# One step of a delta-rule recurrence: the key norm by one wide matmul, masks in wide operations, two heads in turn

## The chip, the cores and the metric

The kernel runs on one core of a Trainium2 chip. The metric is the device time of one execution, in microseconds (us). The kernel before was run three times: 3231.21, 3232.57 and 3237.78 us, with 3232.57 as the median. One further execution was recorded by the hardware profiler; every row below comes from it.

## The reference

A trunk of two layers over 2048 tokens of width 1024, in float32. Layer A is a time-mixing layer with a state of 64 x 64 for each of 12 heads. Layer B is differential attention with 6 heads. Both have a small cross-attention into 256 memory tokens beside them, a gate, an output projection and norms. The change touches layer A alone. What is computed there for every token, cut to what matters:

```
w = -softplus(-(w0 + tanh(wd) @ w2)) - 0.5;  decay = exp(-exp(w))
a = sigmoid(a0 + ad @ a2)
kk = k * k_k;  kk = kk * rsqrt(max(sum(kk * kk, per head), 1e-12))
k = k * (1 + (a - 1) * k_a)
# for each head, token by token:
sa = state @ (-kk)
state = state * decay + sa (kk * a)^T + v k^T
y = state @ r
```

Each head's key direction `kk` is brought to length one (the key norm), and it enters twice: once as `kk` itself and once as `b = kk * a`.

## The kernel before, in words

Layer A goes through 24 steps: two halves of 1024 tokens, in each six pairs of heads, and for each pair two blocks of 512 tokens. In a step the two heads of the pair lie on partitions 0 to 63 and 64 to 127, and the 512 tokens are cut into 8 chunks of 64. Within a chunk the recurrence is solved in closed form, and the state goes from chunk to chunk. A step is traced in these parts.

- p1 (line 312): projections of key, query and value, each 24 matmuls of 128x512 (`pj`, line 174: eight parts of the width, three products of high and low halves); two low-rank products (`lr`, lines 323 and 324: the high part of the weights on all 128 rows, and the low part on 64 of them); decay and gate by exponentials and logarithms on ScalarE, a scan on VectorE (line 330); the key norm (lines 336 to 348); and the tables AR and BK, which hold r, a and k, b of each chunk.
- p2 (line 371): the products `pg` of BK and AR, 64 rows each, for 8 chunks and 2 heads (line 380). A mask for even or odd chunks and the reciprocal norm are put on them on the way out of PSUM (`Gm`, line 383). Then BK is transposed (`bkp`, line 390) and scaled by the reciprocal norm (`BKT`, line 391), and the bonus `pbn` is computed (line 404).
- p3 (line 409): the inverse of a triangular matrix for each chunk and head. Thirty small operations on VectorE solve blocks of 16; two groups of `inv` matmuls (line 455) and the groups `invz` and `invr` (lines 468, 474) join them to 32 and 64.
- p4 (line 482): the recurrence over 8 chunks, one after the other. In a chunk `xy` (lines 493, 496) goes to ScalarE (`xs`), `us` (line 502) to VectorE (`UV`), then come `sps` (line 507), the state's update on VectorE (line 510) and the output `xy` (line 513).
- p5 (line 516): the output's norm, with the transposes `py` (line 535), and its gate.

The scheduler sets the order on every engine when the program is built. While p4 of one step runs, it fills TensorE with the gate projection of that step and the p1 of the step after next (function `filler`, line 584), so `pj` matmuls stand between the short matmuls of p3 and p4. An engine executes its instructions in the order of its row, and whatever waits holds up all that is behind it. The projections, `lr` and `pbn` share three PSUM buffers (tag `pj`); `pg`, `bkp` and the inverse's groups share two others (tag `gm`). The working tiles of 128x512 in SBUF come from eight buffers (tag `w`).

## Time and profile before

| | |
|---|---|
| median of three runs | 3232.57 us |
| lowest and highest run | 3231.21 and 3237.78 us |
| span of the profiled execution | 3242.7 us |
| TensorE (PE) busy | 3074.5 us, 95% |
| VectorE (DVE) busy | 2008.1 us, 62% |
| ScalarE (ACT) busy | 1421.3 us, 44% |
| GpSimd (POOL) busy | 928.4 us, 29% |

The page gives the profiled execution's time as its span, 10.1 us over the median of the other runs. "Busy" is the time in which an engine had at least one instruction in it. Matmuls overlap, and so a TensorE that is busy all the time is not one at its peak. The recorded time of a matmul holds its way through the array too. What one costs in a row of its like is read from start to start.

### The profile page before, as it was taken

How to read it: one execution, taken by the hardware profiler on the slowest of the kernel's cores; microseconds unless marked ns; L12 is line 12 of the kernel's file. 1: busy time of each engine (PE TensorE's matmuls, PEld its weight loads, DVE VectorE, ACT ScalarE, POOL GpSimd, SP SyncE). 2: the span in 40 equal slices, each digit the busy share in tenths (PEclk: the TensorE clock that was granted, in tenths of full speed). 3: DMA queues.
4: the chain of work that ended last, by engine and by line, in shares of the span. 5: the costliest groups of instructions: out<-in, count | busy, mean ns of one | idle time of the engine just before them, and what ended most of it. 6: DMA issues, size and time to landing. Idle time of an engine off the chain costs nothing.

```text
span 3242.7 us, 53751 instructions
## 1 busy us (share of the span) xinstructions
PE 3074.5 (95%) x20026; PEld 2404.1 (74%) x20026; DVE 2008.1 (62%) x5546; ACT 1421.3 (44%) x3126; POOL 928.4 (29%) x1092
## 2 busy tenths in 40 slices
PE   6899999998899999999899999999999999999999
PEld 4766767676667676767577798898887878877777
DVE  6678777866687878786456411111106888887554
ACT  6524333434443434333345522222315777777443
POOL 3224434443244334433100121312411332222100
PEclk9989999998899999999899999999999999999999
DMA  4201000113210001002554443423436555444453
GB/s 131 75 16 35 27 22 22 34 40 90 57 35 27 23 22 33 29 18 69 136 147 135 134 113 90 117 74 96 117 110 159 118 116 112 102 85 119 118 154 113
DMA packets 266150, 265.21 MB, mean 82 GB/s; under 512 B 16832, under 2 KB 206656, under 8 KB 265760
## 3 DMA queue, kind: packets, MB, share of 16 engines
q1 hardware_dynamic: 237760, 195.31, 20.7%
q0 software_dynamic: 28128, 66.46, 10.1%
q8 instruction: 157, 2.57, 0.3%
q14 instruction: 105, 0.86, 0.1%
HBM read 180.45 MB, written 81.26 MB: 81 GB/s over the span
## 4 chain that ended last, share of the span: by engine, by line
PE 76%; DVE 14%; ACT 4%; issue 3%; DMA 2%; POOL 1%; SPq 0%; DVEq 0%; ACTq 0%; POOLq 0%
PE pj L174 30%; PE po L820 10%; PE o L1135 5%; PE vps L996 4%; PE pg L380 3%; PE s L1094 3%; PE s L1095 2%; PE us L502 2%; PE xy L496 2%; PE tr L1125 2%; PE sps L507 1%; PE xy L493 1%; PE mo L759 1%; PE xy L513 1%; DVE E L1097 1%
## 5 line engine op out<-in xcount | busy, mean ns | idle before, releaser
L174 PE MATMUL pj<-hhi,wh 128*128 128x512 f32 x928 | 395.3, 426 | 2.2 <-DVE hlo L149 1.7
L174 PE MATMUL pj<-hhi,wl 128*128 128x512 f32 x928 | 393.2, 424 | 0.4 <-POOL wl L123 0.4
L174 PE MATMUL pj<-hlo,wh 128*128 128x512 f32 x928 | 385.0, 415 | 0.0
L123 POOL TENSOR_TENSOR wl<-wraw,wh 128x512 fp32r<-128x512 f32 x168 | 221.0, 1327 | 399.8 <-ACT wh L122 372.2
L1097 DVE CUSTOM_DVE_ANT_0 E<-s,dist 128x512 f32<-128x512 f32 (+1 forms) x480 | 276.2, 605 | 35.0 <-PE s L1095 28.9
L174 PE MATMUL pj<-bh,wh 128*128 128x512 f32 x672 | 262.6, 391 | 0.0
L174 PE MATMUL pj<-bl,wh 128*128 128x512 f32 x672 | 262.4, 391 | 0.0
L174 PE MATMUL pj<-bh,wl 128*128 128x512 f32 x672 | 262.3, 390 | 0.0
L1102 ACT ACTIVATE E<-E,nm 128x1920 f32<-128x1920 f32 (+7 forms) x192 | 229.4, 1199 | 59.1 <-DVE nm L1100 58.6
L491 POOL TENSOR_SCALAR SP<-sb,PC 128x128 f32<-128x128 f32 x192 | 119.5, 624 | 469.7 <-DVE sb L510 469.7
L1135 PE MATMUL o<-th,vs 128*128 128x256 f32 (+1 forms) x864 | 211.0, 376 | 2.3 <-ACT th L1128 0.9
L174 PEld LDWEIGHTS pj<-hhi,wh 128*128 128x128 f32 x928 | 178.5, 192 | 45.6 <-ACT hhi L148 3.3
L1094 PE MATMUL s<-ks,qd 128*128 128x512 f32 (+1 forms) x480 | 205.7, 432 | 2.2 <-DVE mx L1097 1.2
L174 PEld LDWEIGHTS pj<-hhi,wl 128*128 128x128 f32 x928 | 177.6, 191 | 38.9 <-POOL wl L123 0.8
L174 PEld LDWEIGHTS pj<-hlo,wh 128*128 128x128 f32 x928 | 178.2, 192 | 33.9 <-issue 0.2
L122 ACT ACTIVATE wh<-wraw 128x512 fp32r<-128x512 f32 x168 | 105.4, 628 | 198.0 <-PE pj L174 138.9
L1135 PEld LDWEIGHTS o<-th,vs 128*128 128x128 f32 x864 | 153.8, 189 | 38.7 <-ACT th L1128 19.4
L514 ACT ACTIVATE ys<-xy 64x128 f32<-64x128 f32 x192 | 52.0, 271 | 297.0 <-PE xy L513 251.5
L1095 PE MATMUL s<-ks,qd 128*128 128x512 f32 (+1 forms) x480 | 176.2, 373 | 0.0
L510 DVE SCALAR_TENSOR_TENSOR sb<-sps,PC,SP 64x64 f32<-64x64 f32 x384 | 108.4, 282 | 64.9 <-PE sps L507 57.0
L174 PEld LDWEIGHTS pj<-bh,wh 128*128 128x128 f32 x672 | 126.6, 188 | 26.4 <-DVE ot L831 0.3
L174 PEld LDWEIGHTS pj<-bl,wh 128*128 128x128 f32 x672 | 126.6, 188 | 26.2
(401 smaller groups left out, 7342.3 us busy)
## 6 DMA issues: line engine op xcount, KB each, us to landing
wraw<-in_a_w SPq DMA_DIRECT2D x126, 256.0 KB, 2.9
qd<-qd_d POOLq DMA_DIRECT2D x48, 512.0 KB, 6.9
mq<-mq POOLq DMA_DIRECT2D x64, 256.0 KB, 4.3
ks<-ks_d POOLq DMA_DIRECT2D x24, 512.0 KB, 6.5
yr<-y_dram SPq DMA_DIRECT2D x31, 384.0 KB, 4.9
xt<-in_x SPq DMA_DIRECT2D x16, 512.0 KB, 5.3
x_dram<-ot SPq DMA_DIRECT2D x16, 512.0 KB, 4.4
wraw<-in_b_w SPq DMA_DIRECT2D x32, 256.0 KB, 3.0
```

Source lines behind the costliest of these rows:

```text
L122: A.activation(hi[:, ks], raw, AF.Copy)
L123: eng.tensor_tensor(out=lo[:, ks], in0=raw, in1=hi[:, ks].bitcast(F32), op=ALU.subtract)
L174: mm(ps, lhsT=w[a_][:, k, wcol], rhs=h[b_][:, k, tsl], start=n == 0, stop=n == 3 * KT - 1)
L491: G_.tensor_scalar(out=SP, in0=SB, scalar1=PC[:, c:c + 1], scalar2=None, op0=ALU.mult)
L510: V.scalar_tensor_tensor(out=SB[hc, hc], in0=sp[hc, :], scalar=PC[hc, c:c + 1], in1=SP[hc, hc], op0=ALU.mult, op1=ALU.add)
L820: mm(po[hf], lhsT=a_[:, k, :], rhs=b_[hf][:, k, :], start=k == i == 0, stop=k == KT - 1 and i == 2)
L996: mm(ps[:, t, :], lhsT=hT[b][a_][:, k, tsl], rhs=w[b_][:, k, :], start=n == 0, stop=n == 3 * KT - 1)
L1094: mm(ps[:, f:f + w_], lhsT=qd[:, 0, c, qs], rhs=k_[:, c, 0:w_], start=True, stop=False)
L1095: mm(ps[:, f:f + w_], lhsT=qd[:, 1, c, qs], rhs=k_[:, c, 0:w_], start=False, stop=True)
L1097: V.tensor_tensor_reduce(out=e[:, kb * 512:kb * 512 + w], in0=ps[:, 0:w], in1=dt_[:, u0:u0 + w], scale=-SLOPES[h], scalar=3.0e38, op0=ALU. ...
L1102: A.activation(E[c][:, 0:nk], E[c][:, 0:nk], AF.Exp, bias=nm[:, c:c + 1], scale=-1.0, accum_out=nm[:, 2 + c:3 + c])
L1135: mm(po[:, oc], lhsT=vs[kt // 4][:, kt % 4, :], rhs=th[:, rc], start=n == 0, stop=n >= nmm - 2, skip_group_check=True)
```

## The change

The key norm of p1 no longer ends in a small table. Before, each chunk's squares are multiplied by two columns of ones (`bsum`), which gives sums on the rows of the products, and the reciprocals `rn` scale `Gm` and `BKT`. Now one matmul with `bones`, a 128x128 matrix with a block of ones for each head, gives the sum in every place of a 128x512 tile. A maximum, a logarithm and an exponential make the reciprocal of it, POOL multiplies it with `a`, and the product goes into `b`. The `pg` products then need the mask alone, and four wide operations put it on instead of sixteen. `BKT` becomes a plain copy on ScalarE. The `pg` matmuls of the two heads are issued in turn, into two PSUM tiles. The low part of the `lr` weights stands on all 128 rows. The constants `ones` and `epsd` of layer B get a pool of their own after layer A.

```diff
-                    rows = slice(i * 64, i * 64 + 64)
                     mm(pl, lhsT=lora[:, i], rhs=th[i], start=True, stop=False)
-                    mm(pl, lhsT=lora[rows, 2], rhs=th[i][rows], start=False, stop=True)
+                    mm(pl, lhsT=lora[:, 2 + i], rhs=th[i], start=False, stop=True)
...
-                kk2 = W([P, TB], "kk2")
-                A.activation(kk2, kk, AF.Square)
-                pss = PS([P, NJ, 2], "pss")
-                for c in range(NC):
-                    rows = slice(64, 128) if c % 2 == 0 else slice(0, 64)
-                    mm(pss[rows, c // 2, :], lhsT=kk2[:, c * C:(c + 1) * C], rhs=bsum, start=True, stop=True)
-                rn = T([P, NC, 2], "rn", 3)
-                G_.memset(rn, 1.0)
-                rt = TL([P, NJ, 2], "rt", 2)
-                V.tensor_scalar(out=rt, in0=pss, scalar1=1e-12, scalar2=None, op0=ALU.max)
-                rn4 = rn.rearrange("p (j e) h -> p j e h", e=2)
-                V.reciprocal(out=rn4[64:128, :, 0, :], in_=rt[64:128])
-                V.reciprocal(out=rn4[0:64, :, 1, :], in_=rt[0:64])
+                rn = W([P, TB], "rn")
+                A.activation(rn, kk, AF.Square)
+                pss = PS([P, TB], "pss", "pj")
+                mm(pss, lhsT=bones, rhs=rn, start=True, stop=True)
+                V.tensor_scalar(out=rn, in0=pss, scalar1=1e-12, scalar2=None, op0=ALU.max)
+                A.activation(rn, rn, AF.Ln)
+                A.activation(rn, rn, AF.Exp, scale=-1.0)
+                G_.tensor_tensor(out=rn, in0=rn, in1=asg, op=ALU.mult)
...
-                G_.tensor_tensor(out=kk, in0=kk, in1=asg, op=ALU.mult)
+                G_.tensor_tensor(out=kk, in0=kk, in1=rn, op=ALU.mult)
...
-                for g in range(2):
+                for e in range(2):
+                    pgs = [PS([P, NJ, P], "pg") for hh in range(2)]
+                    for j in range(NJ):
+                        for hh in range(2):
+                            hs = slice(hh * 64, hh * 64 + 64)
+                            mm(pgs[hh][:, j, :], lhsT=BK[hs, 2 * j + e, :], rhs=AR[hs, 2 * j + e, :], start=True, stop=True)
                     for hh in range(2):
-                        pg = PS([P, 4, P], "pg")
-                        hs = slice(hh * 64, hh * 64 + 64)
-                        for c4 in range(4):
-                            c = g * 4 + c4
-                            mm(pg[:, c4, :], lhsT=BK[hs, c, :], rhs=AR[hs, c, :], start=True, stop=True)
-                        for c4 in range(4):
-                            c = g * 4 + c4
-                            V.scalar_tensor_tensor(out=Gm[:, c % 2, c // 2, hh, :], in0=pg[:, c4, :], scalar=rn[:, c, hh:hh + 1],
-                                                   in1=cc("maskE" if c % 2 == 0 else "maskO", 128), op0=ALU.mult, op1=ALU.mult)
+                        V.tensor_tensor(out=Gm[:, e, :, hh, :], in0=pgs[hh], in1=cc(("maskE", "maskO")[e], 128)[:, None, :].broadcast_to([P, NJ, P]), op=ALU.mult)
...
-                    V.tensor_tensor(out=BKT[:, g * 4:g * 4 + 4, :].rearrange("p c (h k) -> p (c h) k", h=2),
-                                    in0=pt.rearrange("p c h k -> p (c h) k"),
-                                    in1=rn[:, g * 4:g * 4 + 4, :].rearrange("p c h -> p (c h)")[:, :, None].broadcast_to([P, 8, 64]), op=ALU.mult)
+                    A.activation(BKT[:, g * 4:g * 4 + 4, :], pt.rearrange("p c h k -> p c (h k)"), AF.Copy)
...
-            l = pw.tile([P, 3, P], F32R, name="lora", tag="lora", bufs=1)
+            l = pw.tile([P, 4, P], F32R, name="lora", tag="lora", bufs=1)
             A.activation(l[:, 0:2], raw, AF.Copy)
-            for i in range(2):
-                rows = slice(i * 64, i * 64 + 64)
-                G_.tensor_tensor(out=l[rows, 2], in0=raw[rows, i], in1=l[rows, i].bitcast(F32), op=ALU.subtract)
+            G_.tensor_tensor(out=l[:, 2:4], in0=raw, in1=l[:, 0:2].bitcast(F32), op=ALU.subtract)
```

The scheduler makes another order of it. The first place is TensorE's row around the end of the inverse, in a step of the first half. Before, `pj` of the query stand among `invz` and `invr`, and the old `pss` follows:

```order
L468 MATMUL invz<-Ta,Gm 32x32 x16
L174 MATMUL pj<-hhi,wl 128x512
L174 MATMUL pj<-hhi,wh 128x512
L174 MATMUL pj<-hlo,wh 128x512
L474 MATMUL invr<-TT,Ta 32x32
L174 MATMUL pj<-hhi,wl 128x512
L474 MATMUL invr<-TT,Ta 32x32 x15
L341 MATMUL pss<-bsum,kk_3241 64x2 x8
```

The same place in TensorE's row of the changed kernel (`py` is the last step's output; L480, L483, L489, L494 and L500 are the recurrence; L320 is `lr`):

```order
L522 MATMUL py<-cvt,ys 128x128 x4
L455 MATMUL invz<-Ta,Gm 32x32 x16
L320 MATMUL lr<-th_1298,lora 128x512
L480 MATMUL xy<-sb_118,AR 128x128
L483 MATMUL xy<-UV,Gm 64x64 x2
L461 MATMUL invr<-TT,Ta 32x32 x16
L489 MATMUL us<-xs,TT 64x64 x2
L494 MATMUL sps<-UV,BKT 64x64 x2
L500 MATMUL xy<-UV,Gm 64x64 x2
L480 MATMUL xy<-sb_120,AR 128x128
L483 MATMUL xy<-UV,Gm 64x64 x2
L335 MATMUL pss<-rn,cvt 128x512
```

Between `invz` and `pss` no `pj` is left. The first chunk of the next step's recurrence and the start of the second stand there, and the 48 `pj` of query and value follow `pss`.

The second place is ScalarE's row for the same part of a step without new weights. Before (`cum` is the decay, `asg` the gate, `kk` the square for the norm, `Ta` the copy between `invz` and `invr`):

```order
L327 ACTIVATE cum<-cum 128x8x64
L457 ACTIVATE E_2963<-inv 128x512
L328 ACTIVATE cum<-cum 128x8x64
L327 ACTIVATE asg<-asg 128x512
L328 ACTIVATE asg<-asg 128x512
L332 ACTIVATE Pt<-cum 128x520
L333 ACTIVATE cum<-cum 128x520
L337 ACTIVATE kk_3241<-kk 128x512
L470 ACTIVATE Ta<-invz 32x256 x2
L279 ACTIVATE rx<-pj,omu 128x512
```

In the changed kernel's row (L333 is the square now, `xs` the recurrence's copy, L524 the output's copy from `py`):

```order
L524 ACTIVATE ys<-py,pvt 128x512
L457 ACTIVATE Ta<-invz 32x256 x2
L323 ACTIVATE cum<-cum 128x8x64
L321 ACTIVATE asg<-lr,nwa 128x512
L324 ACTIVATE cum<-cum 128x8x64
L485 ACTIVATE xs<-xy 64x128
L323 ACTIVATE asg<-asg 128x512
L328 ACTIVATE Pt<-cum 128x520
L324 ACTIVATE asg<-asg 128x512
L329 ACTIVATE cum<-cum 128x520
L333 ACTIVATE rn<-kk 128x512
```

The gate's exponentials and logarithms, which stood in front of `Ta`, stand behind it, and the square is the last of them.

The third place is TensorE's row at the `pg` products. The number in a name is the PSUM tile, one for each head. Before, four of one tile and then four of the next:

```order
L380 MATMUL pg_5289<-AR_5026,BK_5027 128x128 x4
L380 MATMUL pg_5298<-AR_5026,BK_5027 128x128
```

In the changed kernel:

```order
L371 MATMUL pg_5124<-AR_4861,BK_4862 128x128
L371 MATMUL pg_5125<-AR_4861,BK_4862 128x128
L371 MATMUL pg_5124<-AR_4861,BK_4862 128x128
L494 MATMUL sps_4966<-UV_4609,BKT_4596 64x64 x2
L500 MATMUL xy_4956<-UV_4609,Gm_4571 64x64 x2
L371 MATMUL pg_5125<-AR_4861,BK_4862 128x128
```

The two heads take turns, with the recurrence's short matmuls in between as before.

## Rows read from the trace of the kernel before

**Rows 1.** Page, part 1: busy time of each engine, its share of the span, instructions

```profile
PE 3074.5 (95%) x20026; PEld 2404.1 (74%) x20026; DVE 2008.1 (62%) x5546; ACT 1421.3 (44%) x3126; POOL 928.4 (29%) x1092
```

**Rows 2.** Windows by step: length, busy PE, PEld, DVE, ACT, POOL, granted clock, DMA

```profile
1070.70:1122.20 51.50, 49.31 (x427) 35.74 (x427) 41.01 (x124) 18.92 (x42) 18.46 (x24) 1.00 0.04 11
1122.20:1179.60 57.40, 55.06 (x453) 40.05 (x453) 47.27 (x132) 21.73 (x48) 25.48 (x29) 1.00 0.14 40
1179.60:1234.10 54.50, 52.32 (x427) 37.99 (x428) 41.01 (x124) 18.92 (x42) 18.47 (x24) 0.94 0.03 11
```

**Rows 3.** The same view, two short windows inside the third of them

```profile
1184.40:1187.80 3.40, 2.13 (x40) 1.30 (x38) 2.15 (x6) 2.77 (x6) 1.18 (x1) 1.00 0.22 82
1187.80:1194.60 6.80, 6.80 (x58) 5.41 (x58) 4.64 (x12) 0.46 (x1) 3.12 (x3) 0.50 0.00 0
```

**Rows 4.** TensorE's waits, 1013.3 to 1454.9 us: us in all, times, longest

```profile
PE invz L468 <- DVE Ta L461: 7.3, 8, 1.3
PE inv L455 <- DVE T L440: 4.5, 5, 0.9
```

**Rows 5.** Timeline of TensorE: start, us to the last end, instructions merged

```profile
252.26 0.50 PE L323 MATMUL lr<-th,lora 128*128 128x512 f32 x1
252.70 0.50 PE L324 MATMUL lr<-th,lora 64*128 64x512 f32 x1
253.25 0.50 PE L174 MATMUL pj<-hhi,wh 128*128 128x512 f32 x1
...
265.57 0.63 PE L341 MATMUL pss<-bsum,kk 128*64 128x2 f32 x16
266.13 0.50 PE L174 MATMUL pj<-hhi,wl 128*128 128x512 f32 x1
266.47 0.40 PE L174 MATMUL pj<-hhi,wh 128*128 128x512 f32 x1
266.70 0.39 PE L174 MATMUL pj<-hlo,wh 128*128 128x512 f32 x1
...
272.62 1.16 PE L380 MATMUL pg<-AR,BK 64*128 64x128 f32 x10
...
274.07 0.93 PE L380 MATMUL pg<-AR,BK 64*128 64x128 f32 x6
274.93 1.13 PE L404 MATMUL pbn<-kx,rkb 128*128 128x512 f32 x2
275.99 0.34 PE L507 MATMUL sps<-UV,BKT 128*64 128x64 f32 x4
```

**Rows 6.** Groups by line and shape, 200 to 1560 us: busy, mean ns, idle before

```profile
L383 DVE SCALAR_TENSOR_TENSOR Gm<-pg,rn,cvt 128x128 f32<-128x128 f32 x352 | 102.5, 343 | 15.0 <-PE pg L380 12.9
L391 DVE TENSOR_TENSOR BKT<-bkp,rn 128x512 f32<-128x512 f32 x44 | 29.4, 686 | 1.8 <-PE bkp L390 1.3
...
L355 POOL TENSOR_TENSOR kk<-kk,asg 128x512 f32<-128x512 f32 x22 | 28.1, 1276 | 79.7 <-DVE AR L354 37.1 <-DVE PC L362 20.3 <-ACT kk L337 12.2
```

**Rows 7.** Line 330, the scan: shortest, median and longest in ns

```profile
L330 DVE TENSOR_TENSOR_SCAN cum<-cvt,cum x24: 1194/1243/2316, 53.5 to 1461.9; 128x520 f32<-128x520 f32 x24
```

**Rows 8.** Timeline, all engines, one inverse (idle before an instruction in brackets)

```profile
1179.59 1.15 PE L455 MATMUL inv<-T,E 64*64 64x64 f32 x32
...
1180.40 1.07 DVE L444 STREAM_TRANSPOSE TT<-X 128x512 f32<-128x512 f32 x1
...
1184.49 0.66 DVE L458 TENSOR_TENSOR TT<-inv,TT 128x512 f32<-128x512 f32 x1
...
1185.81 0.61 ACT L337 ACTIVATE kk<-kk 128x512 f32<-128x512 f32 x1
...
1186.04 0.69 PE L468 MATMUL invz<-Ta,Gm 32*32 32x32 f32 x32 [1.27 <-DVE Ta L461]
...
1186.77 0.78 ACT L470 ACTIVATE Ta<-invz 32x256 f32<-32x256 f32 x2 [0.35 <-PE invz L468]
...
1189.55 0.85 DVE L476 COPY TT<-invr 32x256 f32<-32x256 f32 x2 [0.46 <-PE invr L474]
```

More of the change, by code (lines that the diff above doesn't have):

```diff
@@ L239, in layer_a @@
         V.tensor_scalar(out=oka, in0=pc("k_a", 0, 6), scalar1=-1.0, scalar2=1.0, op0=ALU.mult, op1=ALU.add)
-        bsum = pa.tile([P, 2], F32, name="bsum")
-        V.tensor_copy(out=bsum[:, 0:1], in_=bones[:, 0:1])
-        V.tensor_copy(out=bsum[:, 1:2], in_=bones[:, 127:128])
         def T(shape, name, bufs=1, tag=None, dt=F32):
@@ L368, in p1 @@
                 mix(pj(ws[2], h), 12 + p, vx)
-                self.rk, self.AR, self.BK, self.PC, self.rn, self.vx = kx, AR, BK, PC, rn, vx
+                self.rk, self.AR, self.BK, self.PC, self.vx = kx, AR, BK, PC, vx
             def p2(self):
-                p, rn, AR, BK = self.p, self.rn, self.AR, self.BK
+                p, AR, BK = self.p, self.AR, self.BK
                 Gm = T([P, 2, NJ, 2, P], "Gm", 2)
-                for g in range(2):
-                    for hh in range(2):
-                        pg = PS([P, 4, P], "pg")
-                        hs = slice(hh * 64, hh * 64 + 64)
-                        for c4 in range(4):
-                            c = g * 4 + c4
-                            mm(pg[:, c4, :], lhsT=BK[hs, c, :], rhs=AR[hs, c, :], start=True, stop=True)
-                        for c4 in range(4):
-                            c = g * 4 + c4
-                            V.scalar_tensor_tensor(out=Gm[:, c % 2, c // 2, hh, :], in0=pg[:, c4, :], scalar=rn[:, c, hh:hh + 1],
-                                                   in1=cc("maskE" if c % 2 == 0 else "maskO", 128), op0=ALU.mult, op1=ALU.mult)
+                for e in range(2):
[4 more added lines that the diff above has]
+                            mm(pgs[hh][:, j, :], lhsT=BK[hs, 2 * j + e, :], rhs=AR[hs, 2 * j + e, :], start=True, stop=True)
+                    for hh in range(2):
+                        V.tensor_tensor(out=Gm[:, e, :, hh, :], in0=pgs[hh], in1=cc(("maskE", "maskO")[e], 128)[:, None, :].broadcast_to([P, NJ, P]), op=ALU.mult)
                 BKT = T([P, NC, P], "BKT", 2)
@@ L1012, in layer_b_proj @@
                         mem_q1(h // 2)
-    ones = const.tile([P, P], F32, name="ones")
-    epsd = const.tile([P, P], F32, name="epsd")
     nlam = const.tile([P, 1], F32, name="nlam")
@@ L1174, in hybrid_kernel @@
     op = layer_a(ph.enter_context(pool_(name="ph", bufs=NB)))
+    const2 = ctx.enter_context(pool_(name="const2", bufs=1, side="right"))
+    ones = const2.tile([P, P], F32, name="ones")
+    epsd = const2.tile([P, P], F32, name="epsd")
     layer_b_proj(ph, op)
```

## The prediction

> **What bounds the kernel now.** I began with the busy line of the page. TensorE is busy 95% of the span, VectorE 62% [rows 1], so a gain has to come out of TensorE's work or its waits. The change touches layer A alone, which is 24 steps of one head pair and 512 tokens, and so I cut that layer into windows from one step's first `inv` matmul to the next one's [rows 2]. Two lengths take turns, 51.50 and 57.40 us. TensorE is busy 49.31 and 55.06 of them, so it waits 2.2 to 2.3 us a step; VectorE is busy 41.0 and 47.3, so it has room. A third window of the short kind takes 54.50 with the same 427 matmuls, at a mean granted clock of 0.94. Cut finer [rows 3], TensorE works 2.13 of 3.40 us, and in the next 6.80 us its granted clock is 0.50, the 1.2 GHz level, though it is busy throughout. Two of the eight steps between 1013.3 and 1454.9 us are like that, and one costs 54.50 - 51.50 = 3.0 us. The list of TensorE's waits over these eight steps [rows 4] puts the largest at `invz` (1.3 us at most) and `inv`: both wait for VectorE inside the triangular inverse (p3). The other links of p3 cost nothing, since `pj` matmuls stand between them.
>
> **What TensorE gains in a step.** All prices are starts in the timeline [rows 5].
> - Products `pg`: a group of ten lasts 1.16 us and a group of six 0.93. The ten have one change of head inside, the six none. Four more matmuls thus cost 0.23, as much as two would at 0.11 each, so at the change of head a matmul of the one head runs beside one of the other. In turn, all 32 should pair: 32 x 0.11 = 3.5 becomes 1.8; groups are cut at odd numbers, so I take 2.0. Gain 1.5 (bounds 0 and 1.75).
> - `lr` (low rank): with 64 rows beside 128 rows, a matmul takes 0.44 and 0.55 to the next start. `pj`, which has the same columns and no change of shape, takes 0.23. Four times 0.45 becomes four times 0.23: gain 0.9.
> - Change of array shape elsewhere: `pj` takes 0.34 to the next start after another shape and 0.23 otherwise, so a change costs 0.11. In the built orders TensorE changes shape 1581 times in layer A before and 1324 times after; 96 of the difference are `lr`'s, counted above. (257 - 96) / 24 = 6.7 a step, gain 0.74.
> - Key norm: sixteen small matmuls, 0.56 to the next start, become one 128x512 product in two passes like `pbn` (1.06), less a change of shape: loss 0.4.
>
> Together 2.75 us a step, 66 us in 24.
>
> **The other engines.** On VectorE sixteen masks of 343 ns become four wide ones. The trace has no such operation. Its bounds are one narrow mask (343) and four of them (1372); I take the 686 ns of `BKT` [rows 6], which has the same shape and also reads PSUM, so 5.5 us become 2.7. `BKT` (two at 686) goes to ScalarE, where a 512 wide operation is 0.61 [rows 8]; the maximum over 512 columns comes in at about 0.7 on VectorE. VectorE loses some 3.5 us a step, ScalarE gains a logarithm, an exponential and two copies, 2.5 us, and POOL one product of 1.28 [rows 6]. The new norm's maximum, logarithm, exponential and two products (about 4.5 us in a row) feed BK, which `pg` needs; I cost that at nothing, since 48 `pj` of 0.23, 11 us, run meanwhile. Without that cover it would be up to 4.5 us a step. VectorE's relief can give back at most the 2.2 us for which TensorE waits at all. The move of `ones` and `epsd` to another pool leaves TensorE's order behind layer A as it was: nothing.
>
> **What it adds: a bare chain.** The order rows in the section on the change show it. Before, `pj` of the query stood between `inv`, `invz`, `invr` and the old `pss`. Now all 48 `pj` of query and value stand behind the new `pss`, in each of the 24 steps. What is left in front of it is waits with almost no cover, and ScalarE has the square last in its row, behind the gate's exponentials. I walk one step without new weights, from the moment when the first `inv` can start (0), with durations of [rows 7, 8]. VectorE has the state update and the second transpose (1.07) and is done at 2.9; `inv` of the second kind ends at 4.2 (1.15); sum (0.66), two products for the output norm and transpose `Ta` to 5.9; `invz` (0.69) from 6.0 to 6.9, behind `py`. ScalarE has the key's copy, an exponential and `py`'s copy before `Ta` (0.78), done at 8.0. `invr` to 8.8, two copies (0.85) to 9.7. ScalarE in the meantime runs a logarithm and two exponentials, and the small `xs` at 9.9, so `us` ends at 10.3. VectorE: minimum, then scan (1.24) from 10.0 to 11.25. ScalarE: four operations of 0.61, the square the last, to 13.6. VectorE and TensorE finish the chunk by 14.1, and `pss` starts there. TensorE's work in these 14.1 us is `inv` 2.2, nine `pj` 2.3, `lr` 0.9, `py`, `invz`, `invr` 2.0, and one chunk and a half of the recurrence 2.9: 10.3. It waits 3.8 here, where the two waits of [rows 4] came to 1.3 + 0.9 at most. In steps with new weights a copy of `lora` and one of `wh` stand in ScalarE's row as well (1.2 us, every second step: 0.6 on the mean). With 0.4 left elsewhere the waits grow from 2.25 to about 4.8, by 2.55. Bounds: nothing, if the fillers reach further than I think, and 3.7, if the scan takes its longest, 2.32 [rows 7].
>
> Work and waits leave -2.75 + 2.55 = -0.2 us a step, about -4 us over 22 steps (the first two differ).
>
> **The clock.** By the walk TensorE works less than 2 of the last 5 us before `pss`, a thinner stretch than the one after which the clock fell [rows 3]; I expect the fall in nearly every step and not in one of four, with the 48 `pj` running into it. It costs between 1.5 (half of the stretch is waiting anyway) and 3.0; I take 2.0. Three quarters of 22 steps are 16: +33 us.
> The Trainium skill (TensorE: Matmul & The Clock Gate, "HAM oscillation") says that idle gaps between bursts of matmuls throttle the engine, and that it starts the next burst cold. It speaks of long gaps. By that rule the clock would not fall here, since no single wait of my walk is over 2 us, and the sum would stop at the -4. In this trace it fell after a wait of 1.3 us at most in a thinly filled stretch, so I follow the rows.
>
> Sum: -4 + 33 = +29 us. The profiled execution has a span of 3242.7 us, which becomes 3272. It stands 10.1 us over the median of the runs (3232.57), so the runs should show about 3261.
>
> **Rivals.**
> 1. The work saved comes through. For it: TensorE's busy share, and waits of only 2.2 us now. Against it: 48 `pj` behind `pss` in every step. If VectorE's relief makes the chain end early, 2.75 x 24 = 66 us go: 3167; with half of it 3200. Decides from waits below 3.5 us a step.
> 2. Savings and waits cancel, and the clock holds, as in six of the eight steps now: -4, 3229, give or take 10.
> 3. Deeper on the slow side: the fall takes the whole 3.0 (16 x 3.0 = 48), and the scan has its long form in every step (2.32 - 1.24 = 1.08, x 22 = 24): -4 + 48 + 24 = +68, 3301. It decides where `pss` starts later than 15 us after the first `inv`. The same end is reached if the change does not do what it says, because the two heads' products, though in turn, do not pair (22 x 1.5 = 33 on top of my +29: 3295). Against that: the ten and the six.
>
> **How the numbers follow.** A difference under 0.2% (6.5 us) can't be told from none: the three runs lie 6.6 us apart. Forecast 0.45 (3239 to 3290), rival 1 0.27 (3165 to 3226), rival 2 0.14, rival 3 0.14. Rival 1 is all faster; rival 2 is split between faster 0.04, same 0.08 and slower 0.02; the forecast gives 0.03 to same. Faster 0.31, same 0.11, slower 0.58. The range reaches from a little below the half of rival 1 (3185) to a little over rival 3 (3320); outside stand the better half of rival 1 and a few in 100 above. The forecast's own range is 3239 to 3290.
>
> **What would show it.** Steps: windows between first `inv` matmuls of about 55 to 57 us on the mean, granted clock under 0.97 in most of them. In the `pg` groups every second start should follow within some nanoseconds, and `lr` should take 0.23. The new `pss` starts about 14 us after the first `inv`, and TensorE's largest waits are `us`, `sps` and `pss` just before it. I am wrong if TensorE's waits a step stay at 2 us, or if the clock stays at 1.00 in most steps.

## The result and the profile after

The changed kernel takes 3308.61 us (median of three runs, 3308.13 to 3310.18) against 3232.57. The ratio is 1.0233, with an interval of 1.0215 to 1.0252. The forecast was 3261: the direction was right, and +76 us came where +29 were forecast. The spans of the two profiled executions differ by 64.1 us (3242.7 and 3306.8): the one before stands 10.1 us over its median, the changed one 1.8 us under its own. The busy line of the changed kernel's page, which answers to [rows 1]:

```profile
PE 3078.1 (93%) x19690; PEld 2423.0 (73%) x19690; DVE 1941.1 (59%) x5160; ACT 1466.5 (44%) x3222; POOL 964.4 (29%) x1080
```

TensorE has fewer matmuls to do and is busy for longer. The view by windows, first over eight steps of the kernel before (window, length, busy PE, PEld, DVE, ACT, POOL, granted clock, DMA):

```profile
1013.30:1454.90 441.60, 423.60 (x3506) 307.59 (x3506) 352.95 (x1017) 162.82 (x356) 175.78 (x206) 0.98 0.09 27
```

and of the changed kernel: the same eight steps, two steps among them, and one of these two in three parts.

```profile
1044.90:1508.50 463.60, 426.07 (x3396) 314.59 (x3394) 331.69 (x888) 178.27 (x388) 187.45 (x204) 0.93 0.09 25
...
1102.90:1160.40 57.50, 53.04 (x426) 39.60 (x426) 40.47 (x111) 20.15 (x44) 18.20 (x22) 0.91 0.02 6
1160.40:1219.90 59.50, 53.79 (x416) 39.44 (x417) 43.05 (x110) 24.26 (x52) 28.61 (x29) 0.91 0.15 43
...
1102.90:1111.80 8.90, 7.49 (x119) 5.97 (x118) 7.54 (x21) 4.75 (x10) 2.99 (x6) 0.99 0.01 2
1111.80:1122.00 10.20, 7.75 (x54) 5.51 (x55) 4.78 (x10) 5.79 (x11) 1.25 (x2) 0.50 0.07 27
1122.00:1160.40 38.40, 37.81 (x255) 28.11 (x254) 28.15 (x80) 9.61 (x24) 13.96 (x15) 1.00 0.00 1
```

A step takes 57.95 us on the mean (463.60 / 8) instead of 55.20 (441.60 / 8). TensorE waits 37.5 us in eight steps (463.60 - 426.07) instead of 18.0. The last three rows show where: the step's first 19.1 us hold 3.9 of its 4.5 us of waits and the whole fall of the clock, and the 38.4 us behind them are nearly full and at 1.00. All eight steps have such a fall, of 6.8 or 10.2 us, four of each; before, two of eight had one, of 6.8 us [rows 2, 3].

The timeline of TensorE through that stretch (start, us to the last end, instructions merged, in brackets the idle time and what ended it):

```profile
1109.25 0.44 PE L483 MATMUL xy<-UV,Gm 64*64 64x64 f32 x4
1109.80 0.69 PE L455 MATMUL invz<-Ta,Gm 32*32 32x32 f32 x32
1112.10 1.46 PE L461 MATMUL invr<-TT,Ta 32*32 32x32 f32 x32 [1.61 <-ACT Ta L457]
1115.24 0.69 PE L489 MATMUL us<-xs,TT 64*64 64x64 f32 x4 [1.68 <-DVE TT L463]
1116.31 0.48 PE L494 MATMUL sps<-UV,BKT 128*64 128x64 f32 x4 [0.39 <-DVE UV L490]
1116.58 0.63 PE L500 MATMUL xy<-UV,Gm 128*64 128x64 f32 x4
1117.14 2.08 PE L335 MATMUL pss<-rn,cvt 128*128 128x512 f32 x2
1118.23 1.42 PE L174 MATMUL pj<-hhi,wh 128*128 128x512 f32 x1
1119.44 0.63 PE L174 MATMUL pj<-hlo,wh 128*128 128x512 f32 x1
```

TensorE's waits over the eight steps, which answer to [rows 4] (us in all, times, longest; five of the eight lines):

```profile
PE sps L494 <- DVE UV L490: 6.9, 10, 0.9
PE xy L480 <- DVE sb L497: 6.2, 9, 1.3
PE us L489 <- ACT xs L485: 6.1, 4, 1.6
PE us L489 <- DVE TT L463: 5.2, 4, 1.7
PE invr L461 <- ACT Ta L457: 5.2, 8, 1.6
```

In the timeline the clock is at half from 1111.8 on: `invr`, `us`, `pss` and the first `pj` run slowly (a `pj` recorded with 0.63 where [rows 5] have 0.39). `pss` starts 14.3 us after the first `inv` (14.3 to 15.0 over the eight steps); the walk of the prediction had 14.1.

**The step split in three.** Over these eight steps I summed the matmuls from start to start. *Waits* is time with no matmul under way. What matmuls took in half-clock stretches above what their like takes at full clock is *clock loss*; the rest is *work*. The like is the same matmul between the same neighbours. `pss` and the `pj` behind it ran slowly in all eight steps, 2.30 us from the start of `pss` to the start of the second `pj` (1117.14 to 1119.44); their like is taken from the version `fill` below, whose clock held, with 1.19:

```profile
1113.94 1.12 PE L337 MATMUL pss<-rn,cvt 128*128 128x512 f32 x2 [0.29 <-ACT rn L333]
1114.50 0.79 PE L174 MATMUL pj<-hhi,wh 128*128 128x512 f32 x1
1115.13 0.40 PE L174 MATMUL pj<-hlo,wh 128*128 128x512 f32 x1
```

| us a step | work | waits | clock loss | step |
|---|---|---|---|---|
| before | 52.20 | 2.25 | 0.75 | 55.20 |
| changed | 50.25 | 4.69 | 3.01 | 57.95 |
| difference | -1.95 | +2.44 | +2.26 | +2.75 |
| forecast | -2.75 | +2.55 | +1.5 | +1.3 |

Waits outweigh the work saved by 0.5 us a step, and the clock adds 2.26: over 22 steps 11 and 50 us, of the 64. That stretches eight steps over 22. By windows, the sixteen steps of the two regular stretches hold 45.2 of the 64.1 us, the four around the turn of the halves 5.7, what lies ahead of the third step 2.7, and the last two steps with all behind them 10.5.

### The profile page after: what moved, and what is told of

Same layout as the page of the kernel before. It is cut to its first block, busy times and chain, and to the rows that moved or that the text cites. A ratio compares the mean times of both kernels' runs of the same rounds, so it can differ in the third digit from the quotient of the medians.

```text
span 3306.8 us, 52684 instructions
## 1 busy us (share of the span) xinstructions
PE 3078.1 (93%) x19690; PEld 2423.0 (73%) x19690; DVE 1941.1 (59%) x5160; ACT 1466.5 (44%) x3222; POOL 964.4 (29%) x1080
## 4 chain that ended last, share of the span: by engine, by line
PE 78%; DVE 12%; ACT 5%; issue 2%; DMA 1%; SPq 0%; POOL 0%; DVEq 0%; ACTq 0%; POOLq 0%
PE pj L174 33%; PE po L805 9%; PE o L1118 5%; PE vps L981 4%; PE s L1077 3%; PE s L1078 2%; PE pg L371 2%; PE tr L1108 2%; PE inv L442 2%; PE us L489 2%; PE xy L483 2%; PE pss L335 1%; PE sps L494 1%; PE xy L480 1%; PE mo L744 1%
## 5 line engine op out<-in xcount | busy, mean ns | idle before, releaser
L174 PE MATMUL pj<-hhi,wh 128*128 128x512 f32 x928 | 415.2, 447 | 4.1 <-DVE hlo L149 2.1
L174 PEld LDWEIGHTS pj<-hhi,wh 128*128 128x128 f32 x928 | 184.8, 199 | 57.7 <-issue 12.6
L174 PEld LDWEIGHTS pj<-hlo,wh 128*128 128x128 f32 x928 | 183.9, 198 | 48.3 <-issue 12.4
L174 PEld LDWEIGHTS pj<-bh,wl 128*128 128x128 f32 x672 | 126.5, 188 | 26.2
```

The lines of the kernel that those rows point to most:

```text
L174: mm(ps, lhsT=w[a_][:, k, wcol], rhs=h[b_][:, k, tsl], start=n == 0, stop=n == 3 * KT - 1)
```

## The experiments

Eighteen kernels were run, each beside runs of the kernel before on the same chip. All of them in one table: median, mean granted clock over the runs, and the split of eight steps of one profiled execution. On these chips the kernel before had medians of 3229 to 3237 us, so medians of two versions from different chips, if they differ by 8 us or less, can't be told apart. The expectations use a rougher split (clock loss 0.65 before and 3.3 after).

| version | us | clock | work | waits | clock loss |
|---|---|---|---|---|---|
| before | 3233 | 0.979 | 52.2 | 2.3 | 0.8 |
| changed | 3309 | 0.954 | 50.3 | 4.7 | 3.0 |
| pss_gm | 3312 | 0.952 | 50.1 | 4.4 | 3.9 |
| q_first | 3303 | 0.954 | 50.4 | 4.0 | 3.3 |
| norm_early | 3311 | 0.951 | 50.3 | 4.0 | 3.4 |
| short_path | 3309 | 0.953 | 50.3 | 4.7 | 3.0 |
| short_q | 3288 | 0.957 | 50.4 | 3.7 | 3.5 |
| fill8 | 3295 | 0.965 | 51.8 | 3.3 | 2.1 |
| fill | 3286 | 0.980 | 53.6 | 2.6 | 0.0 |
| norm_only | 3318 | 0.950 | 51.5 | 3.4 | 3.1 |
| no_norm | 3271 | 0.966 | 51.5 | 3.2 | 3.1 |
| turn | 3264 | 0.969 | 52.1 | 2.8 | 1.8 |
| lora_alone | 3237 | 0.976 | 51.6 | 2.5 | 0.9 |
| fill_before | 3276 | 0.976 | 53.6 | 2.3 | 0.9 |
| p3_after | 3263 | 0.958 | 49.4 | 3.9 | 2.6 |
| p3_before | 3227 | 0.971 | 51.5 | 2.0 | 3.7 |
| gate_after | 3324 | 0.950 | 50.5 | 4.2 | 5.6 |
| both_after | 3236 | 0.963 | 49.4 | 3.3 | 2.0 |
| invz_before | 3267 | 0.976 | 53.3 | 2.2 | 0.4 |
| invz_no_norm | 3259 | 0.979 | 52.8 | 2.8 | 0.4 |

(The profiled execution of p3_before was 30 us over its median, at a clock of 0.962; its clock loss is too high by that. p3_after has the matmuls of the changed kernel and 0.9 us a step less work: their order alone moves the work by as much.)

**Where `pss` stands.** My first theory was that the place of `pss` alone leaves TensorE bare.

```diff
 pss_gm:
-                pss = PS([P, TB], "pss", "pj")
+                pss = PS([P, TB], "pss")
 q_first, ahead of the tile pss:
+                pr_ = pj(ws[1], h)
...
-                mix(pj(ws[1], h), p, rx)
+                mix(pr_, p, rx)
```

> The changed kernel, with one edit: the PSUM tile of the norm product pss is taken from the two buffers of tag gm (those of pg, bkp and the inverse) instead of the three of tag pj. In TensorE's built order the pj of the query then stand again between invz, invr and pss, some 25 of them, and the 48 pj no longer stand behind pss. Theory 1 (the place of pss makes a thin stretch, in which TensorE waits and after which the clock falls): waits back to about 2.3 us a step from 4.1, falls in a quarter of the steps, the 2.75 us of work saved come through at least by half: 3165 to 3200 us, mean clock 0.975 or more. Theory 2 (what costs is in the operations themselves: wide masks, the norm's longer chain through ScalarE and POOL, not where pss stands): within 20 us of the changed kernel, 3290 to 3325, clock 0.95 as there.

> The changed kernel, with the query's projection (24 pj) traced ahead of pss, and only its copy out of PSUM left where it was. pss keeps its PSUM tag. In the built order about 24 pj stand among invz and invr and pss follows them. Theory 1 (thin stretch in front of pss): as the version with pss in the other buffers, 3165 to 3215 us, clock 0.97 or more. Theory 2 (the operations themselves): 3290 to 3325. If this one gains and the one with other buffers doesn't, it is the cover alone that counts; if the reverse, the buffer ring that pss holds.

Both medians stay within 6 us of the changed kernel's; the theory fell. TensorE's waits in eight steps of q_first, and two of its windows:

```profile
PE pg L372 <- DVE BK L352: 23.0, 8, 3.6
PE sps L495 <- DVE UV L491: 4.7, 4, 1.2
```

```profile
1160.70:1222.60 61.90, 56.21 (x417) 40.44 (x416) 45.26 (x112) 24.64 (x52) 29.34 (x30) 0.86 0.14 41
1222.60:1275.80 53.20, 51.03 (x433) 37.36 (x432) 40.72 (x112) 19.93 (x45) 18.37 (x21) 1.00 0.02 6
```

The waits ahead of `pss` are gone, and TensorE now waits for BK, behind `pss`: 23.0 us in eight steps, up to 3.6 at once. In pss_gm it is 22.6 and 3.8. The clock falls there as well, some 26 us after the first `inv`. The 24 `pj` of the query can cover the chain in front of `pss` or the norm's path behind it, but not both.

**Idle matmuls over the bare stretch.**

```diff
 fill (fill8: range(8)):
                 pss = PS([P, TB], "pss", "pj")
+                for k in range(16):
+                    mm(pss, lhsT=ws[1][0][:, k % KT], rhs=h[0][:, k % KT], start=True, stop=True)
                 mm(pss, lhsT=bones, rhs=rn, start=True, stop=True)
```

> The changed kernel with 16 more matmuls of 128x512 a step, which are written into the tile of pss just ahead of its own matmul and overwritten by it: work whose result is not used. At 0.23 us each at full clock they are 3.7 us a step, 88 us in 24 steps, if they stand beside nothing. Theory 1a (the fall of the clock is the price, and it is the thin stretch in front of pss that makes it): the clock goes back to 0.975 or more, each step wins 3 to 4 us of clock and loses 3.7 less the part that lies in waits (1.9 of them): 3240 to 3310 us, not slower than the changed kernel although TensorE has 88 us more work. Theory 1b (waits are the price, clock a by-product that follows the load elsewhere): clock stays at 0.95, 3340 to 3400. Theory 2 (the operations themselves): 3350 to 3400 as well.

> The changed kernel with 8 idle matmuls a step into pss instead of 16. Work 1.85 us a step more than the changed kernel. If the clock holds as with 16 (loss 0 instead of 3.3 us) and half of what 16 took from the waits (2.1) is gone, a step takes 57.95 + 1.85 - 3.3 - 1.0 = 55.5 us: 3308 - 22 x 2.45 = 3254 us (3240 to 3270). If 8 are too few and the fall stays in every step: 57.95 + 1.85 - 1.0 = 58.8 us, 3320 to 3330. In between, if it goes in half of the steps.

Two neighbouring steps of fill:

```profile
1041.20:1099.90 58.70, 53.97 (x440) 38.85 (x440) 46.51 (x112) 24.51 (x53) 30.10 (x30) 1.00 0.15 44
1099.90:1153.80 53.90, 53.37 (x443) 39.55 (x443) 39.63 (x113) 19.79 (x44) 18.14 (x21) 1.00 0.02 6
```

and of fill8:

```profile
1099.00:1151.30 52.30, 51.53 (x435) 37.98 (x435) 39.78 (x113) 19.79 (x44) 17.86 (x21) 1.00 0.02 6
1151.30:1215.70 64.40, 58.59 (x432) 42.07 (x431) 46.00 (x111) 24.39 (x53) 29.58 (x30) 0.87 0.14 40
```

With 16 x 0.23 = 3.7 us more of useless matmuls a step the kernel is 22 us faster than the changed one, and no clock falls in these eight steps. A step of them takes 1.7 us less (56.25): 3.4 more work, 2.1 less waits, 3.0 less clock loss. That is shown: the falls hang on the bare stretch, and the work filled in there is paid for by waits and clock together. It is not shown for every step. In the first half's eight steps three falls are left, at 29 to 30 us, and these steps take as long as the changed kernel's (465.90 us against 466.30):

```profile
250.80:716.70 465.90, 444.85 (x3523) 324.07 (x3522) 342.48 (x890) 177.40 (x388) 192.32 (x204) 0.96 0.08 25
```

With eight the clock holds in the steps without new weights and falls in the others, at 27 to 30 us.

**Parts alone.** norm_only keeps the norm in front of b, the wide masks and BKT's copy on ScalarE, and undoes the pairs and `lr`; no_norm does the reverse; turn and lora_alone are the kernel before with one of these two each.

```diff
 norm_only (on the changed kernel):
-                    for j in range(NJ):
-                        for hh in range(2):
+                    for hh in range(2):
+                        for j in range(NJ):
...
-                    mm(pl, lhsT=lora[:, 2 + i], rhs=th[i], start=False, stop=True)
+                    rows = slice(i * 64, i * 64 + 64)
+                    mm(pl, lhsT=lora[rows, 2], rhs=th[i][rows], start=False, stop=True)
...
 turn (on before; no_norm adds the lr edit, lora_alone is the lr edit alone):
                 for g in range(2):
+                    pgs = [PS([P, 4, P], "pg") for hh in range(2)]
+                    for c4 in range(4):
+                        c = g * 4 + c4
+                        for hh in range(2):
+                            hs = slice(hh * 64, hh * 64 + 64)
+                            mm(pgs[hh][:, c4, :], lhsT=BK[hs, c, :], rhs=AR[hs, c, :], start=True, stop=True)
                     for hh in range(2):
-                        pg = PS([P, 4, P], "pg")
...
+                        pg = pgs[hh]
```

> The changed kernel with two of its parts undone: the pg products of a head stand together again (four of one head, then four of the other, for even and for odd chunks), and the low part of the lr weights stands on 64 rows as before. What is left of the change is the norm in front of b, the wide masks and BKT on ScalarE. In the built order the chain from inv to pss is as bare as in the changed kernel. Theory 3 (the norm in front of b makes a longer serial path in every step, for which there is not enough other work; where TensorE is bare follows from it, and pairs and lr have no part in it): waits 4.7 us a step and a fall of the clock in every step as in the changed kernel, and 1.5 us a step more work (0.8 of pairs, 0.7 of lr): 3308 + 22 x 1.5 = 3340 us, 3320 to 3350. Theory 4 (less work of TensorE is what uncovers the chain; with more work the waits fill): 3235 to 3300, clock over 0.965.

> The kernel before with the heads of pg in turn, the low part of lr on 128 rows and the constants in their own pool, but with the small norm table, the narrow masks and BKT as before. In the built order pj stand among inv, invz and invr again. Theory 3 (the norm in front of b): waits 2.3 to 2.8 us a step, clock loss as with heads in turn alone (1.8 us a step) or less, work 0.7 less than there: 3215 to 3255 us. Theory 4 (less work of TensorE uncovers the chain): slower than heads in turn alone (3264), 3265 to 3300.

> The kernel before, with only the pg products of the two heads issued in turn into two PSUM tiles; norm, masks, lr and all else as before. My pricing by rows: 32 products go from 3.5 to 2.0 us a step, so -1.5 x 24 = -36 us, 3195 to 3205 if TensorE's work comes through; 3225 to 3240 if the time saved turns into waits for VectorE's masks; over 3250 if in this kernel too less work of TensorE ends in more falls of the clock.

> The kernel before with only the low part of the lr weights on all 128 rows (and the constants in their own pool): 0.7 us a step less work of TensorE, nothing else on any engine changes. If TensorE's work sets the pace: 3232 - 24 x 0.7 = 3217 us (3210 to 3222). If work and waits always add up to 54.5 (theory 6): within 6 us of before, or slower by up to 30 us through more falls of the clock: 3230 to 3262.

norm_only has a fall in every step: the norm in front of b is enough for it, together with the wide masks and BKT's copy, which no version takes apart from it. It came out faster than expected, because its waits were 3.4 and not 4.7. But the other parts are no gain either, and no_norm came out where theory 4 had it. turn is 0.85% slower than before (interval 0.64 to 1.06), no_norm 1.2% (0.98 to 1.38), and lora_alone, which changes nothing but 0.6 us of TensorE's work a step, is 0.12% slower (0.01 to 0.22). Why turn waits more is in VectorE's row. Of the kernel before, between the inverse's sum `TT` and its transpose `Ta`:

```profile
1073.37 2.31 DVE L330 TENSOR_TENSOR_SCAN cum<-cvt,cum 128x520 f32<-128x520 f32 x1
1075.61 0.66 DVE L458 TENSOR_TENSOR TT<-inv,TT 128x512 f32<-128x512 f32 x1
1076.19 0.47 DVE L335 TENSOR_SCALAR kk<-kx,pvt 128x512 f32<-128x512 f32 x1
1076.58 0.43 DVE L461 STREAM_TRANSPOSE Ta<-TT 128x256 f32<-128x256 f32 x1
```

and of turn:

```profile
1132.74 0.68 DVE L460 TENSOR_TENSOR TT<-inv,TT 128x512 f32<-128x512 f32 x1
1134.10 1.24 DVE L330 TENSOR_TENSOR_SCAN cum<-cvt,cum 128x520 f32<-128x520 f32 x1 [0.69 <-ACT cum L328]
1135.26 0.42 DVE L463 STREAM_TRANSPOSE Ta<-TT 128x256 f32<-128x256 f32 x1
```

The scheduler put the scan, which waits for ScalarE, between the two. `Ta` comes 2.52 us after `TT` instead of 0.97, `invz` waits 13.0 us in eight steps instead of 7.3 [rows 4], and four of the eight steps have a fall.

**A shorter path for the norm.**

```diff
 norm_early: the block from kk to the second exponential stands behind the key's mix, ahead of lr
 short_path (short_q: the same on q_first):
-                G_.tensor_tensor(out=rn, in0=rn, in1=asg, op=ALU.mult)
...
-                G_.tensor_tensor(out=kk, in0=kk, in1=rn, op=ALU.mult)
-                V.tensor_tensor(out=slots(BK, True), in0=q4(kk), in1=Pi4, op=ALU.mult)
+                G_.tensor_tensor(out=kk, in0=kk, in1=asg, op=ALU.mult)
+                G_.tensor_tensor(out=q4(kk), in0=q4(kk), in1=Pi4, op=ALU.mult)
+                V.tensor_tensor(out=slots(BK, True), in0=q4(kk), in1=q4(rn), op=ALU.mult)
```

> The changed kernel with the block of the norm (square, pss, maximum, logarithm, exponential) traced right behind the key's projection and ahead of lr and the scan; only its product with a stays behind. pss then follows invr directly in TensorE's row, and the square no longer stands behind the gate's exponentials. The 48 pj still stand behind pss. Theory 3: a shorter path, pss some 2 to 4 us earlier, waits 3 to 4 us a step instead of 4.7, falls of the clock in some of the steps: 3240 to 3295 us. If the chain from inv to invr alone is thin enough for the fall, and what was waiting in front of pss now waits elsewhere: 3295 to 3325.

> The changed kernel with the same shorter path from pss to pg, and the query's pj behind pss as there. The 48 pj of 11 us already hide that path in the changed kernel, so by theory 5 nothing is gained: 3300 to 3315. By theory 6 also within 15 us of the changed kernel. A gain of more than 20 us would say that the changed kernel's path behind pss was late after all.

> The version with the query's 24 pj ahead of pss, with a shorter path from pss to pg: POOL multiplies the key with a and with the decay ahead of the norm, and after the exponential there is one product on VectorE into BK, where two on POOL (1.28 us each) and one on VectorE stood. In that version TensorE waits 3.6 us a step for BK in front of pg in every second step, and the clock falls there. Theory 5 (the norm's path in front of BK is what leaves TensorE bare): that wait goes to 1 to 1.5 us, waits 3.0 a step instead of 4.0, clock loss 1 to 2 us instead of 3.5: 3215 to 3270 us. Theory 6 (work and waits of TensorE always add up to about 54.5 us a step, since a chain through the other engines sets the pace, and whatever leaves TensorE's row comes back as a wait): the wait turns up at another place, 3285 to 3315.

norm_early and short_path changed nothing; in short_path that was expected. short_q's median is 15 us under q_first's, 9 if each is set against the kernel before on its own chip, and the two intervals overlap: less than theory 5 wanted, and inside theory 6's range. Its waits say why:

```profile
PE pg L372 <- DVE AR L357: 12.6, 4, 3.2
PE pg L372 <- DVE BK L348: 8.3, 4, 2.1
```

BK holds `pg` for 8.3 us instead of 23.0, but AR, the next in VectorE's row, for 12.6.

**Less work on VectorE and ScalarE, more on TensorE.** These ask whether a path through the other engines sets the pace. The p3 and gate versions leave out operations and compute something else than the reference.

```diff
 p3_after, p3_before:
-                for j in range(15):
+                for j in range(5):
 gate_after (both_after: with the edit above):
-                    V.tensor_scalar(out=e, in0=e, scalar1=BIG, scalar2=None, op0=ALU.min)
-                    A.activation(e, e, AF.Ln, bias=1.0)
 fill_before (on before):
-                mix(pj(ws[1], h), p, rx)
+                pr_ = PS([P, TB], "pj", "pj")
+                for k in range(6):
+                    mm(pr_, lhsT=ws[1][0][:, k % KT], rhs=h[0][:, k % KT], start=True, stop=True)
+                proj(pr_, ws[1], h, slice(0, TB))
+                mix(pr_, p, rx)
```

> The changed kernel without 20 of the 30 small VectorE operations of a step's triangular inverse (the inverse is left incomplete, so its output is not the reference's): 20 x 0.24 = 4.8 us less in VectorE's chain, TensorE's work as it is. Theory 6: work and waits fall from 54.6 to 50.5 to 52 us a step, TensorE is covered again, the clock loss goes to 1 or less: 3308 - 22 x (3 to 6.5) = 3165 to 3240 us. Theory 5 (it is the chain from lr over the scan to pss and on to BK, which these operations only precede): waits stay at 4 or more and the clock falls in every step, 3270 to 3315.

> The kernel before without the same 20 operations (output not the reference's). Theory 6: TensorE's work of 52.3 us is the floor then, waits fall from 2.25 to 1 us or less, the clock loss of 0.65 to 0.3: 3232 - 22 x 1.6 = 3197 us (3185 to 3215). The distance of the two kernels then turns round: the changed one is faster by up to 2.4 us a step. If TensorE waits for something else, within 10 us of 3232.

> The changed kernel without the minimum on VectorE and the logarithm on ScalarE of both gates between lr and the scan (0.7 and 0.6 us each; output not the reference's). TensorE's work as it is. If this path to pss sets the pace: the sum of work and waits falls by 1.3 to 2.6 us a step, the clock loss stays at about 3: 3308 - 22 x (1.3 to 2.6) = 3250 to 3280 us. If only the triangular inverse counts (the version without 20 of its operations, 3263): 3300 to 3312.

> The changed kernel without those four gate operations and without the 20 operations of the triangular inverse (output not the reference's). If both places are parts of one path that sets the pace, their gains add up: 3263 less what the gates alone give, 3205 to 3240 us, and by the point where waits are under 2.5 us a step the clock comes back as well: down to 3150. If one path hides behind the other: 3250 to 3263.

> The kernel before with 6 idle matmuls a step, written into the query's pj tile and overwritten by it. In the built order they stand in front of invz, TensorE's longest wait, and just where its clock falls in every fourth step. 1.4 us a step more work. Theory 6: part of it lies in the waits (2.25 go to 1.3 or so), the clock loss of 0.65 goes to 0: 3232 + 22 x (1.4 - 0.95 - 0.65) = 3228 us, 3218 to 3240, clock 0.983 or more. If TensorE's work sets the pace: 3232 + 24 x 1.4 = 3266 us, less what the clock gives back, 3245 to 3266.

Without some 4.8 us of VectorE work a step (20 x 0.24) the changed kernel is 46 us faster, between the ranges of theories 5 and 6, and for the kernel before no difference can be told (ratio 0.9953 to 1.0011). So the changed kernel does hang on VectorE's path more than the kernel before, but its clock keeps falling. Without the gates' operations alone it is 15 us slower, outside both ranges expected, with 14 falls in eight steps. Without both it is 73 us faster, more than the two edits add up to (46 - 15): why isn't shown. fill_before missed its aim. In most steps the built order puts the idle matmuls ahead of the first `inv` and not in front of `invz`, whose wait of 1.27 us stays. Its timeline:

```profile
1091.57 1.64 PE L366 MATMUL pj<-hhi,wh 128*128 128x512 f32 x6
...
1095.73 1.15 PE L459 MATMUL inv<-T,E 64*64 64x64 f32 x32
...
1102.18 0.69 PE L472 MATMUL invz<-Ta,Gm 32*32 32x32 f32 x32 [1.27 <-DVE Ta L465]
```

It shows only that such work is not repaid where the row is full: 1.4 us a step more work are 33 us in 24 steps, and the kernel is 42 us slower, above both ranges expected.

**Idle matmuls bound to their place.** Two more kernels tie them to the stretch in front of `invz` by an operand, the sum TT, from which `Ta` is made.

```diff
 invz_before (invz_no_norm, on no_norm: range(3)):
                 pz = PS([P, NJ, 2, 32], "invz")
+                for k in range(2):
+                    mm(pz.rearrange("p j h t -> p (j h t)"), lhsT=bones, rhs=TT.rearrange("p j h t -> p (j h t)")[:, 0:256], start=True, stop=True)
```

> The kernel before with two idle matmuls a step into the PSUM tile of invz, overwritten by it: bones by the first 256 columns of TT, so they can't start before the sum TT and stand directly in front of invz in TensorE's row, in the built order in every step. Some 0.5 us each in two passes, 1.1 us a step more work. If the stretch in front of invz is what lets the clock fall: falls gone from it, loss 0.65 to 0.1; the wait for Ta goes from 0.9 a step to nearly nothing, but the three pj that the scheduler moves away stand elsewhere: 3234 + 22 x (1.1 - 0.9 - 0.5) = 3227 us, 3212 to 3240, clock 0.983 or more. If the falls do not hang on that stretch: 3245 to 3265, clock 0.979 or less.

> The version with the old norm, heads in turn and lr on 128 rows (3271 us: work 51.8, waits 3.2, clock loss 2.9), with three idle matmuls a step at the same place, 1.6 us. If the stretch in front of invz is what lets the clock fall: the wait of 1.65 us a step for Ta is filled and the clock loss goes to 0.7 or less: 3271 - 22 x (2.2 to 2.9) = 3207 to 3223 us, faster than the kernel before. If not: 3275 to 3305.

In invz_no_norm one of eight steps has a fall (at 46 us) where no_norm has seven (six of them at 8 to 9.5 us), and the steps of the first half go from six falls to one. So in the regular steps the stretch in front of `invz` lets the clock fall in these versions. The time hardly follows. With 1.2 us a step more work invz_no_norm is 12 us under no_norm, 9 if each is set against the kernel before on its own chip, and the intervals of the two ratios overlap (1.0081 to 1.0111 and 1.0098 to 1.0138); 48 us or more were expected. In invz_before the falls at 8 to 9 us are gone too, but it is 1.1% slower than before, at a clock of 0.976, close to what was expected if the falls do not hang on that stretch (3245 to 3265). Of the 31 us between its profiled execution and the one before, 15.6 stand in the four steps around the turn of the halves, where the clock fell more often (7 times for 4). The waits did not go, either. In invz_no_norm:

```profile
PE invz L466 <- DVE TT L460: 6.8, 8, 1.1
...
PE invz L472 <- DVE Ta L463: 3.5, 5, 0.7
```

L466 are the idle matmuls. They now wait for TT, since the scheduler moved some `pj` from in front of them to other places; no_norm waits 13.2 us at `invz` in eight steps, this one 6.8 + 3.5.

**The price of the clock, from runs of one program.** Executions of the same program differ in their clock. Over 151 runs of the 20 kernels, each set against its own kernel's mean, 0.001 less of mean clock goes with 2.34 us more (interval 2.20 to 2.47). The kernel before has 0.979 (57 runs), the changed one 0.954 (3 runs): 25 x 2.34 = 59 us of the 76, where the split gave 50 for 22 steps. By this estimate, which takes the price inside one program for the price between two, the changed kernel would be some 16 us slower at equal clock, turn and no_norm some 8, lora_alone 4 faster: none of the work taken from TensorE came through beyond that.

## Why the prediction was right in sign and short in size

- **Bare chain.** Right in its size: waits 4.69 us a step (4.8 forecast), the largest at `us` (11.3 in eight steps) and `sps`, as named; at `pss` itself there is little, and `xy` and `invr` take its place. ([rows 4] leave out that `sps` waited 4.5 us before, too, as much as `inv`.) That `pss` starts at 14.3 us, where the walk had 14.1, is in part luck. The walk had `us` end at 10.3 and TensorE wait for the square at the end of ScalarE's row. In the profile the scan (`cum` L326) stands on VectorE in front of the copies of TT that `us` needs, and `us` starts 12.4 us after the first `inv`. The chain there:

```profile
1111.67 0.37 ACT Ta L457
1112.07 0.39 ACT Ta L457
1112.47 0.64 ACT cum L324
1113.20 1.24 DVE cum L326
1114.44 0.30 DVE TT L463
1114.76 0.43 DVE TT L463
1115.24 0.70 PE us L489 x4
```

- **TensorE's work: a step that failed.** -1.95 us a step came where -2.75 were forecast, 18 us in 22 steps. What is missing is mostly `pg`, which gave 0.76 and not 1.5: two heads' products start 6 or 7 ns apart in 10 pairs of 16 in six of the eight steps, in 8 in the other two (2 before). I took it that all would pair. Behind the first tiles the built order runs one head alone in places, probably because that head's tile comes free before the other's; that isn't shown. In the timeline six with pairs take 0.71 where six without took 0.93 [rows 5]:

```profile
1131.94 0.71 PE L371 MATMUL pg<-AR,BK 64*128 64x128 f32 x6
...
1136.16 0.71 PE L371 MATMUL pg<-AR,BK 64*128 64x128 f32 x4
1137.17 0.94 PE L371 MATMUL pg<-AR,BK 64*128 64x128 f32 x10
```

  `lr` gave 0.68 (0.9); changes of shape and the rest, less the new `pss`, gave 0.5 (0.3).
- **VectorE.** The wide mask took 687 ns, as the 686 taken for it, and VectorE is busy 2.7 us a step less (3.5 forecast).
- **The norm's path at nothing.** Right while 48 `pj` stand behind `pss`. q_first measured what it costs without half of them: 2.9 us a step, under the bound of 4.5.
- **The clock: the other step that failed.** I put it at 16 more falls of 2.0 us, +33. The number was right: eight of eight steps have one where two had, 16.5 more in 22. The price was not: 50 / 16.5 = 3.0 us each, the top of my bounds. I took the price from one window, [rows 2], where a fall of 6.8 us cost 3.0, and went under it because half of the slow stretch would be waiting anyway. In the changed kernel the falls of 6.8 us cost 2.4 to 3.0 us. The other four last 10.2 us: they begin 9 us after the first `inv`, in front of `invr` and not of `pss`. They do hold over 2 us of waits, and cost 3.2 to 3.5 all the same: the chain's own matmuls run at half speed in them, and `pss` and the first `pj` as well. By the rule of the Trainium skill (TensorE: Matmul & The Clock Gate, "HAM oscillation") long idle gaps throttle the engine. No single wait here was over 1.7 us, and the clock fell in every step: this trace, like [rows 3], does not need a long gap.
- **The profiled execution.** I took off 10.1 us for the distance of the span from the median. The changed kernel's span stands 1.8 us under its median, and so 12 us of the miss are this term's. The rest of the 47 us (3309 against 3261) is 17 of the clock, 18 of TensorE's work, and small terms.
- **Rivals.** Rival 1 needed waits under 3.5 us; they were 4.7. Rival 2 had work and waits at -4, where they came to +11, and the wrong clock. Rival 3's 3301 was nearest, and in two of its terms right: the fall took its 3.0 (50 us, 48 by the rival), and half of the pairs did not come. Its sign did not show: `pss` was not later than 15 us, and the scan took 1.24.

What stays open is whether any order of this kernel lets the 2 us of saved work come through. None of the versions beat the kernel before with its output whole. And what exactly ties the number of falls to the order (14 in eight steps in gate_after) isn't shown, beyond that covering two such stretches (fill, invz_no_norm) stopped most of the falls there.

## What to carry to other kernels

Split a step into work, waits and clock loss before pricing an edit. In a row that is covered by a fixed stock of filler matmuls, less work and a longer serial path both show up as waits, and each such stretch can then cost about as much in clock again (here 2.3 us a step beside 2.4 of waiting). A stock of filler covers one place: before a value is put onto the path of its consumer (here the norm in front of b), count what is left to cover the place that it leaves.

## What the runs showed of the hardware

- Useless matmuls paid for themselves: 89 us of them (24 x 3.7) made the changed kernel 22 us faster (3309 to 3286), with its mean clock up from 0.954 to 0.980.
- One program's runs can differ by 1.4% with the clock (p3_before: 3211 us at 0.981, 3257 at 0.962).
- Matmuls on the two halves of the rows start 6 or 7 ns apart when they alternate, with 105 ns to the next pair, and 112 ns apart when they don't.
